# A window of eight loads on the loading queue of a squared-distance kernel

## The chip, the cores and the metric

One core of a Trainium2 chip. The metric is the device time of one execution in microseconds (us), which is some 1.35 us longer than the span of the profile. SP (SyncE) is the engine that here only waits and issues loads. A load counts as landed when the last of its 16 parts, which the trace records one by one, has arrived; a semaphore counts the parts up to 16.

## The reference

```python
x, y: float32 [1024, 4096]
np.sum((x - y) ** 2, axis=-1).astype(np.float32)     # 1024 results
```

33.55 MB are read once, 4 KB are written.

## The kernel before

Each of the 128 partitions holds eight rows of x and of y (8 x 4096 columns). SP issues 18 loads, cut into pieces of very different size; VectorE subtracts, ScalarE squares and sums. The buffers X and Y hold six rows each, so most of the loads from load 5 on reuse the place of rows 0 and 1, and SP issues them only when ScalarE has squared row 1.

```python
    H = 6 * D                                   # columns in each of the buffers X and Y
    xw = [4096, 12288, 8192, 5472, 1280, 960, 320, 160]
    yw = [16256, 8192, 2624, 2784, 1344, 480, 480, 288]
    late, last = 128, 192                       # two more small y loads, issued at the end
    ...
    def load(landed, src, dst, name, c0, c1):
        sem = prog.semaphore("%s%d" % (name, len(landed)))
        nc.sync.dma_start(out=dst[:, home(c0, c1)], in_=src[:, c0:c1]).then_inc(sem, 16)
        landed.append(((c0, c1), sem))
    ...
    todo = list(order)
    load(*todo.pop(0))
    prog.early(mybir.EngineType.SP)
    while todo and todo[0][5] <= H:             # the first block: loads 0 to 4
        load(*todo.pop(0))
    ...
            squared[piece] = n["acts"]
            if r in (0, 1):
                nc.sync.wait_ge(acts, n["acts"])
                while todo and todo[0][5] <= H + (r + 1) * D:
                    load(*todo.pop(0))
                if r == 1:                      # the second block: loads 5 to 17
                    while todo:
                        load(*todo.pop(0))
```

In issue order the loads have 2048, 6144, 8128, 4096 and 4096 KB (0 to 4), then 2736, 1312, 1392, 640, 672, 480, 240, 240, 160, 144, 80, 96 and 64 KB (5 to 17). Every load has its own semaphore, and VectorE waits for the loads of a piece before it subtracts.

## Time and profile before

| | before |
|---|---|
| median of the first 3 runs | 84.03 us (84.0 to 84.2) |
| span of the profile | 82.6 us |
| VectorE / ScalarE busy | 36.8 / 33.4 us |
| share of the span that the DMA engines are busy | 95.9% |
| last load landed | 80.25 us |

In the view of DMA issues, each line has the tensor, the issuing queue, the count, the size of one and the time from issue to landing; these are the lines for loads 13 to 17 of the kernel before:

```profile
X<-in_x_dram SPq DMA_DIRECT2D x1, 160.0 KB, 21.9
Y<-in_y_dram SPq DMA_DIRECT2D x1, 144.0 KB, 20.6
Y<-in_y_dram SPq DMA_DIRECT2D x1, 96.0 KB, 13.1
X<-in_x_dram SPq DMA_DIRECT2D x1, 80.0 KB, 15.6
Y<-in_y_dram SPq DMA_DIRECT2D x1, 64.0 KB, 12.8
```

A load of 64 KB that takes 12.8 us is not slow: it stands in a queue. The DMA row of the kernel before, for the stretch from 74 to 80.3 us alone (40 slices, busy tenths):

```profile
DMA  9999997999969999999899999999999999996000
```

There is work on the DMA engines up to 79.8 us. If the change lets the queue run empty, that row must show it.

### The profile page before, as it was taken

The page shows a single profiled execution, that of the slowest core. Times are in us where ns is not written, and L with a number is a line of the kernel's source. Part 1 is how long each engine was busy: PE and PEld are TensorE (multiplying, and loading weights), DVE is VectorE, ACT ScalarE, POOL GpSimd, SP SyncE. Part 2 cuts the span into 40 slices and gives each one's busy share as a digit, 9 for nine tenths or more (in the row PEclk, how much of TensorE's full clock was granted, in tenths as well). Part 3 has the DMA queues.
Part 4 walks back from the last instruction along what each step waited for, and adds up shares of the span by engine and source line. Part 5 has one row for each costly group of instructions (what it writes and reads, how often), then busy time and mean ns, then how long its engine had stood idle before and what let it go on. Part 6 is the DMA issues. An engine that isn't in the chain of part 4 may idle for free.

```text
span 82.6 us, 136 instructions
## 1 busy us (share of the span) xinstructions
DVE 36.8 (45%) x27; ACT 33.4 (40%) x41; POOL 0.2 (0%) x4
## 2 busy tenths in 40 slices
DVE  0000000000000000000299999999189996989992
ACT  3300000000000000000000979889896999899991
POOL 0000000000000000000000000000000000000000
DMA  5998998888999991999599699969979799999960
GB/s 127 389 500 381 595 547 381 381 381 381 504 504 504 504 504 63 441 504 504 254 508 508 286 476 508 476 286 508 423 339 509 339 437 440 426 402 416 395 220 2
DMA packets 2736, 33.56 MB, mean 406 GB/s; under 512 B 432, under 2 KB 1328, under 8 KB 1712
## 3 DMA queue, kind: packets, MB, share of 16 engines
q1 hardware_dynamic: 2736, 33.56, 95.9%
HBM read 33.55 MB, written 0.00 MB: 406 GB/s over the span
## 4 chain that ended last, share of the span: by engine, by line
DMA 63%; SPq 16%; DVE 12%; ACT 4%; issue 1%
DMA Y<-in_y_dram 63%; SPq L108 16%; DVE X L175 11%; ACT X L181 4%; DVE Y L204 0%; DVE results L188 0%; SPq L220 0%; DVE results L204 0%
## 5 line engine op out<-in xcount | busy, mean ns | idle before, releaser
L175 DVE TENSOR_TENSOR X<-X,Y 128x2048 f32<-128x2048 f32 (+10 forms) x21 | 36.2, 1780 | 44.3 <-DMA Y<-in_y_dram 44.3
L181 ACT ACTIVATE X<-X 128x2048 f32<-128x2048 f32 (+9 forms) x20 | 31.2, 1559 | 46.1 <-DVE X L175 46.0
L181 ACT ACTIVATION_READ_ACCUMULATOR X<-X 128x1 f32 x20 | 3.7, 186 | 0.0
L181 ACT ACT_TABLE_LOAD x1 | 1.3, 1283 | 1.4 <-PEq L19 1.4
L188 DVE TENSOR_REDUCE results<-parts 128x1 f32<-128x2 f32 (+2 forms) x4 | 0.4, 152 | 0.0
L204 DVE CUSTOM_DVE_ANT_0 Y<-X,parts 128x128 f32<-128x128 f32 x1 | 0.4, 352 | 0.0
L250 POOL MEMSET const-bfloat16-1.0<- 128x1 bf16 x1 | 0.1, 101 | 0.0
L250 POOL MEMSET const-uint8-127<- 128x1 uint8 x1 | 0.1, 101 | 0.0
L250 POOL MEMSET const-float32-0.0<- 128x1 f32 x1 | 0.1, 98 | 0.2 <-issue 0.2
L250 POOL MEMSET const-float32-1.0<- 128x1 f32 x1 | 0.1, 98 | 0.0
L204 DVE DVE_READ_ACCUMULATOR2_ANT results<- 128x1 f32 x1 | 0.1, 83 | 0.0
## 6 DMA issues: line engine op xcount, KB each, us to landing
Y<-in_y_dram SPq DMA_DIRECT2D x1, 8128.0 KB, 39.0
X<-in_x_dram SPq DMA_DIRECT2D x1, 6144.0 KB, 20.2
X<-in_x_dram SPq DMA_DIRECT2D x1, 4096.0 KB, 48.3
Y<-in_y_dram SPq DMA_DIRECT2D x1, 4096.0 KB, 57.5
X<-in_x_dram SPq DMA_DIRECT2D x1, 2736.0 KB, 13.3
X<-in_x_dram SPq DMA_DIRECT2D x1, 2048.0 KB, 7.1
Y<-in_y_dram SPq DMA_DIRECT2D x1, 1392.0 KB, 19.0
Y<-in_y_dram SPq DMA_DIRECT2D x1, 1312.0 KB, 16.1
```

Of the source, the lines that this page charges most:

```text
L108: nc.sync.dma_start(out=dst[:, home(c0, c1)], in_=src[:, c0:c1]).then_inc(sem, 16)
L175: nc.vector.tensor_sub(out=a, in0=a, in1=Y[:, home(c0, c1)]).then_inc(diffs, 1)
L181: nc.scalar.activation(out=a, in_=a, func=Square, accum_out=acc).then_inc(acts, 1)
L188: nc.vector.tensor_reduce(out=results[:, r : r + 1], in_=parts_of(r, len(row_parts[r])), axis=mybir.AxisListType.X, op=add,).then_inc(sums, 1)
L204: nc.vector.tensor_tensor_reduce(out=Y[:, home(*piece)], in0=X[:, home(*piece)], in1=X[:, home(*piece)], scale=1.0, scalar=parts_of(r, 1), ...
L250: nc = _bacc.Bacc("TRN2", target_bir_lowering=False, num_devices=1)
```

## The change

No load is issued before the load eight places ahead of it has landed. The intent is a bounded number of loads under way. Sizes, order, buffers and compute stay as they were.

```diff
-    landed_x, landed_y = [], []
+    landed_x, landed_y, issued = [], [], []
+
+    AHEAD = 8
     freed = []

     def load(landed, src, dst, name, c0, c1):
+        if len(issued) >= AHEAD:
+            nc.sync.wait_ge(issued[-AHEAD], 16)
         sem = prog.semaphore("%s%d" % (name, len(landed)))
+        issued.append(sem)
         nc.sync.dma_start(out=dst[:, home(c0, c1)], in_=src[:, c0:c1]).then_inc(sem, 16)
```

## The prediction

> **What bounds the kernel now.** I read the page first: engine shares, the 40 slices, the DMA part, the chain that ended last.
>
> ```profile
> DVE 36.8 (45%) x27; ACT 33.4 (40%) x41; POOL 0.2 (0%) x4
> DMA  5998998888999991999599699969979799999960
> q1 hardware_dynamic: 2736, 33.56, 95.9%
> HBM read 33.55 MB, written 0.00 MB: 406 GB/s over the span
> DMA 63%; SPq 16%; DVE 12%; ACT 4%; issue 1%
> ```
>
> VectorE and ScalarE are each under half busy; the 16 DMA engines are busy 95.9% of the span. The chain is mostly DMA. Its 16% of "SPq L108" look like an issue cost, so the question is whether SP's issuing holds anything up. The chain in order of time, from the second block of loads on, together with SP's timeline:
>
> ```profile
> 57.17 0.04 issue
> 57.22 1.69 SPq L108
> 58.91 0.04 issue
> 58.95 5.21 SPq L108
> 64.16 0.04 issue
> 64.20 2.69 SPq L108
> 66.89 0.04 issue
> 66.94 13.12 DMA Y<-in_y_dram
> 80.05 0.02 issue
> 80.08 0.57 DVE X L175 x2
> ```
>
> An ordinary issue takes 0.44 us (the timeline has 0.43 to 0.46 for those between 54 and 57 us). From 57.2 us on, single issues take 1.69, 5.21 and 2.69 us, and the line's own view gives 5.57 us for the last one. So SP is already being held: something in front of it is full. That is part of the chain only because the chain is followed through issues; the loads issued so late still wait 13 us for their turn. What counts is when each load lands. I number the 18 loads in issue order, 0 to 17, and add "us to landing" (DMA issues view; sizes identify the loads) to the issue's start (timeline):
>
> - 0 to 4 (2048, 6144, 8128, 4096, 4096 KB), issued in the first 3.2 us, land at 7.1, 21.7, 40.8, 50.6 and 60.3.
> - 5 (2736 KB) 53.45 + 13.3 = 66.8; 6 (1312) 53.8 + 16.1 = 69.9; 7 (1392) 54.3 + 19.0 = 73.3; 8 (640) 54.8 + 20.0 = 74.8; 9 (672) 55.3 + 21.1 = 76.4; 10 (480) 77.5; 11 (240) 78.2; 12 (240) 78.7; 13 (160) 79.1; 14 (144) 79.6; 15 (80) 64.2 + 15.6 = 79.8; 16 (96) 66.9 + 13.1 = 80.05; 17 (64) 67.4 + 12.8 = 80.2.
>
> They land strictly in issue order. Load 5 takes 66.8 - 60.3 = 6.5 us after load 4 for 2.80 MB, which is 431 GB/s; 6 and 7 take 3.1 and 3.4 us, about 420 to 430 GB/s; the small ones at the end fall towards 330 to 410 GB/s (loads 10 to 17, 1504 KB = 1.54 MB, between 76.4 and 80.2: 405 GB/s). The stretches by time agree: 437 GB/s from 41 to 53 us, 407 to 426 from 53 to 73. So one queue, served in order at its full rate, sets the end; after the last landings there are 0.57 us of subtraction, 0.35 us of the fused square and sum, the reduce, and the 1.4 us store.
>
> **What the Trainium skill says.** (1) "DMA: Bandwidth & Descriptors", section "Anatomy of one DMA — SWDGE (gpsimd) path": DMA engines do not wait on semaphores; a wait is held on the issuing sequencer ahead of dispatch, and the engines just consume their queues. So the added wait costs SP time and costs DMA time only if a queue runs empty. The trace agrees: SP stood at a wait for ACT for 50.2 us in all (the DMA queue's own waits) while DMA stayed at 9 tenths. (2) Same page, "Queues, rings and completion order": on each engine descriptors are consumed in ring order, but the 16 engines finish independently and completion is not promised in order. This matters, since a wait for a full landing is a wait for the slowest engine: with engines far apart, a quick one could empty its share of eight loads while a slow one holds the ninth back. The landing records of this trace show the 16 parts of one load within 0.2 to 0.25 us of each other (load 7: 73.01 to 73.25), in issue order, so there is no such spread. (3) Same page, "Specifications": fabric ceiling 435 GB/s. The trace shows 437 GB/s at best over 12 us, so the queue has no rate to gain. (4) Same page, "Latency and other measured facts": first byte of a hardware-issued DMA about 0.6 us. The trace bounds it from above: the 4 KB store took 1.4 us from issue to landing.
>
> **The change, part by part.** Nothing is removed; sizes, order, buffers and compute stay. Added: for loads 8 to 17, ten waits on SP, load i waiting for the landing of load i-8. SP computes nothing. Between the semaphore and the next instruction the chain shows 0.02 to 0.05 us, so ten satisfied waits would be about 0.4 us of SP time, off the path.
>
> When does each wait end, taking the landings above? Loads 0 to 3 have landed before the second block starts at 53.45, so loads 8, 9, 10 and 11 go as now. The others:
> - 12 waits for 4: 60.3 instead of 56.7.
> - 13 waits for 5: 66.8 instead of 57.2.
> - 14 waits for 6: 69.9 instead of 58.95.
> - 15 waits for 7: 73.3 instead of 64.2.
> - 16 waits for 8: 74.8 instead of 66.9.
> - 17 waits for 9: 76.4 instead of 67.4.
>
> So six loads are issued 3.6 to 11 us later. Does the queue run dry? Queue ahead at each of these moments, in KB: at 12, loads 5 to 11 = 2736 + 1312 + 1392 + 640 + 672 + 480 + 240 = 7472, 18 us of work; at 13, loads 6 to 12 = 4976; at 14, loads 7 to 13 = 3824; at 15, loads 8 to 14 = 2576; at 16, loads 9 to 15 = 2016, 5.0 us; at 17, loads 10 to 16 = 1440 KB = 1.47 MB, about 3.7 us (76.4 to 80.05). A new issue needs 0.44 us on SP and some start-up. Upper estimate for both: 1.4 us, the whole store. A more cautious one: load 0 took 7.1 us for 2.10 MB, where 435 GB/s would need 4.8, so 2.3 us of cold start. Load 17 is then in its queue by 77.8 (78.7 cautiously), and its turn comes at 80.05: margin 2.3 us (1.35). Load 16: in by 76.2 to 77.1, turn at 79.8, margin 2.7 or more. All earlier ones have more. So no landing moves.
>
> What is gained: the long issues. With at most eight loads in the queue the 1.69, 5.21, 2.69 and 5.57 us should all fall to about 0.44. (The long ones began with some ten loads outstanding: the 14th was issued with 4 to 12 ahead, the 18th finished at 73.0 with 8 to 16 and a piece of 7 ahead.) But this is SP time in which SP had nothing else to do; the next thing it does is the store at 81.18. Worth on the path: 0.
>
> Sum: DMA +0, VectorE and ScalarE +0, SP off the path, tail +0. 84.03 + 0.0, to which I add 0.02 for nothing more than the run spread of 84.0 to 84.2: **84.05 us**.
>
> **The rivals.**
> - *The queue runs dry at the end.* For it: the last loads are small, and waiting for a whole load's landing makes the window eight loads and not so many bytes. Against it: 1440 KB are still ahead at the tightest point. If the start-up were 5 us instead of at most 2.3, load 17 would land about 1.5 us late and the time would be 85 to 85.5; over 2% (1.7 us) would need more still. 3%.
> - *A shorter queue is served better*, because SP no longer pushes against a full one. For it: the rate falls from 437 GB/s (41 to 53 us, no issues) to 407 from 53 to 60 us when the second block is issued. Against it: rows get shorter there too, and the landings from 60 to 73 us, in the very time of the held issues, are at 420 to 431 GB/s. At the most the 1504 KB after 76.4 would go at 430 instead of 405 GB/s: 0.2 us, giving 83.8. A gain over 2% would need the whole stream above the best rate seen. 1%.
> - *A shorter queue is served worse*: engines that look ahead in their queue find less. Only the last few us have a short queue, and it is never empty; at the cost of, say, 5% over loads 10 to 17 (3.8 us) this is 0.2 us, giving 84.25. 10%.
>
> **Range and chances.** The mechanism says equal; the two small rivals are 0.2 us either way and the spread of runs 0.2 us. So 83.8 to 84.35. Faster by over 2% (under 82.35): 0.01. Within 2%: 0.97. Slower (over 85.7): 0.02.
>
> **What would show it.** In the profile after: issues of loads 12 to 17 start near 60.3, 66.8, 69.9, 73.3, 74.8 and 76.4, each about 0.44 us long, with no long SP issue left; their times to landing shrink to about 18, 12, 10, 6.5, 5 and 4 us (now 22, 22, 21, 16, 13 and 13) while the landings themselves stay within 0.3 us, the last near 80.2. The waits of SP show landings of DMA as releasers; the chain's "SPq L108" shrinks from 16% and DMA takes its place. Queue share stays near 96%, span near 82.6. Wrong if the DMA row shows a gap between 76 and 80 us, if load 17 lands over 4.5 us after its issue, or if the landings from 60 us on come at another rate than 420 to 431 GB/s.

## The result, and the profile after

After: 84.15 us median (84.07 to 84.24, six runs), before 84.13 us (84.0 to 84.2, six runs). The ratio is 1.0005, 95% interval 0.9992 to 1.0018. A ratio here is the mean time of one kernel's fast runs over that of the other's in the same rounds, so it is not quite the ratio of the medians.

The page of the kernel after: the DMA row of the whole span, the queue's share, the bytes, the chain that ended last.

```profile
DMA  5999999888999994799799899989999899999950
q1 hardware_dynamic: 2736, 33.56, 95.5%
HBM read 33.55 MB, written 0.00 MB: 405 GB/s over the span
DMA 78%; DVE 12%; ACT 4%; SPq 2%; issue 1%
```

The engines of the DMA are as full as they were. In the chain SP's queue fell from 16% to 2% and DMA rose from 63% to 78%, with no time gained: the chain only follows the last load back through another release, now a landing and not a string of issues.

SP's timeline after, loads 12 to 17 and the store (start, duration; "x2" merges two issues with what lies between, in the first line loads 11 and 12):

```profile
56.53 4.35 SPq L113 DMA_DIRECT2D Y<-in_y_dram  x2
67.03 0.33 SPq L113 DMA_DIRECT2D X<-in_x_dram  x1
70.19 0.33 SPq L113 DMA_DIRECT2D Y<-in_y_dram  x1
73.51 0.33 SPq L113 DMA_DIRECT2D X<-in_x_dram  x1
75.05 1.93 SPq L113 DMA_DIRECT2D Y<-in_y_dram  x2
81.44 0.35 SPq L237 DMA_DIRECT2D out_dram<-results  x1
```

The issues of 1.69, 5.21, 2.69 and 5.57 us are gone; each of these six loads is issued in 0.33 us (load 12 at 60.55, load 17 at 76.65 in the records). SP's waits, after:

```profile
SPq L113 <- DMA Y<-in_y_dram: 10.6, 4, 3.5
SPq L113 <- DMA X<-in_x_dram: 7.3, 2, 6.1
SPq L237 <- DVE results L193: 4.4, 1, 4.4
```

So 17.9 us of waits for landings (six waits) took the place of 13.4 us of holding: the four long issues less 0.44 us each. Where SP stands still has changed its name. The loads' times from issue to landing, after:

```profile
X<-in_x_dram SPq DMA_DIRECT2D x1, 160.0 KB, 12.4
Y<-in_y_dram SPq DMA_DIRECT2D x1, 144.0 KB, 9.6
Y<-in_y_dram SPq DMA_DIRECT2D x1, 96.0 KB, 5.2
X<-in_x_dram SPq DMA_DIRECT2D x1, 80.0 KB, 6.5
Y<-in_y_dram SPq DMA_DIRECT2D x1, 64.0 KB, 3.8
```

They fell by 8 to 11 us, and the end didn't move, because only the time that a load stands in the queue has shrunk. The DMA row from 74 to 80.3 us, after:

```profile
DMA  9999899999999999989999999999999999987310
```

No gap: the row stays at 8 or 9 up to 79.6 us and falls where that of before falls too. The landings, from the landing records (time at which the last of the 16 parts of a load landed):

| load | issued before | landed before | issued after | landed after | landing moved by |
|---|---|---|---|---|---|
| 0 | 0.00 | 7.12 | 0.00 | 7.36 | +0.24 |
| 4 | 2.77 | 60.27 | 2.81 | 60.53 | +0.26 |
| 7 | 54.30 | 73.25 | 54.56 | 73.50 | +0.25 |
| 9 | 55.26 | 76.38 | 55.57 | 76.64 | +0.26 |
| 12 | 56.73 | 78.75 | 60.55 | 79.00 | +0.25 |
| 15 | 64.20 | 79.79 | 73.51 | 80.02 | +0.23 |
| 17 | 67.41 | 80.25 | 76.65 | 80.46 | +0.21 |

The profiled execution after has a span of 82.9 us, 0.3 us more than before. That isn't the change: the 0.24 us stand already at load 0, which was issued long ahead of the first added wait, and they stay the same to the end. It is a difference between two executions, and the six runs of each kernel don't show it.

### The profile page after: what moved, and what is told of

It reads as the page before. It is cut to its first block, busy times and chain, and to the rows that moved or that the text cites. A ratio compares the mean times of both kernels' runs of the same rounds, so it can differ in the third digit from the quotient of the medians.

```text
span 82.9 us, 136 instructions
## 1 busy us (share of the span) xinstructions
DVE 36.8 (44%) x27; ACT 33.4 (40%) x41; POOL 0.2 (0%) x4
## 4 chain that ended last, share of the span: by engine, by line
DMA 78%; DVE 12%; ACT 4%; SPq 2%; issue 1%
DMA Y<-in_y_dram 54%; DMA X<-in_x_dram 24%; DVE X L180 11%; ACT X L186 4%; SPq L113 2%; DVE Y L209 0%; DVE results L193 0%; SPq L225 0%; DVE results L209 0%
```

## The experiments

The prediction rests on a margin: a late issue costs nothing as long as the work ahead of it outlasts its start-up. To test it I made the margin vanish in several ways, and worked out what each should cost by a recurrence: landing(i) = max(landing(i-1), landing(i-A) + S) + own time of i. Here A is the window, and the own times are the differences between the landings of before. S, the start-up, is what a load costs from its release to its landing beyond its own time. Four kernels ran first, four more and then two more later, all of them correct; the first eight ran on one chip and share most of their runs of before, the last two ran on another chip with new runs of before. Each ratio is against these runs of before (median 84.14 us for all).

**One load waits for the load just ahead.** AHEAD's lines are replaced:

```diff
-        if len(issued) >= AHEAD:
-            nc.sync.wait_ge(issued[-AHEAD], 16)
+        if len(issued) == 17:
+            nc.sync.wait_ge(issued[16], 16)
```

> Only load 17 (64 KB) waits, and for the landing of load 16, the load just ahead of it; loads 8 to 16 go without the added wait. Its queue is then empty, so its start-up S (from the semaphore that releases it to its first bytes arriving) lies open on the path. My theory (a wait costs DMA time only when the queue runs dry, S between 1.4 and 2.3 us): load 17 lands about 1.4 to 2.3 us later than now relative to load 16, the end by nearly as much (the reduce waits for load 17's piece): 85.4 to 86.3 us. Rival (later issue is hidden anyway, since the engines prefetch or the tail has slack): within 0.3 us of before.

Measured: 85.5 us, ratio 1.0167 (1.0143 to 1.0192), so 1.4 us more. Its chain has load 17 as

```profile
80.24 1.73 DMA Y<-in_y_dram
```

Load 17 was released at 80.22, when load 16 landed, and landed at 81.97; less its own 0.20 us, S is 1.55 us on an idle queue. The end moved by less than the landing, since VectorE's subtraction of load 16 was done meanwhile. The rival (late issues are hidden whatever is ahead) falls.

**Windows of 1, 2 and 4.** `AHEAD = 8` becomes 1, 2, 4.

> AHEAD = 1, one load at a time, each after the landing of the one before. My theory: 17 loads show S each: 17 x 1.4 = 24 us to 17 x 2.3 = 39 us more, 108 to 123 us; the gaps between landings each grow by the same S whether the load is big or small. Rival (a shorter queue is served better or worse in itself): the rate of the big loads 1 to 5 changes too, beyond the constant S.

Measured: 118.15 us, ratio 1.4055. From load 0 to load 17, 107.43 us pass and not 73.13: 34.3 us more over 17 loads, 2.0 us each. The chain of ahead_1, in order of time, three of its loads:

```profile
7.15 16.92 DMA X<-in_x_dram
...
96.55 3.13 DMA X<-in_x_dram
...
112.74 1.82 DMA Y<-in_y_dram
```

Load 1 (6144 KB, rows of 48 KB) takes 16.92 us and had 14.53 of its own: S is 2.4 us. Load 10 (rows of 3.75 KB): 3.13 less 1.16, 2.0 us. Load 17 (rows of 512 B): 1.82 less 0.20, 1.6 us. The total was as expected, but "the same S whether the load is big or small" was wrong: S grows with the length of the rows. No run was made to separate why, but the records of the packets (one packet is one row of one load) show where the growth sits. In each of loads 1 to 17 the first packet starts 0.94 to 0.97 us after the issue, and the landing comes 0.28 to 0.39 us after the end of the last packet, whatever the size. What grows is the time of the first 16 packets of a load, those after the pause: 2.5 us on average with rows of 48 KB, where the others take 1.8 us as in before; 0.35 us with 3.75 KB, where the median is 0.15; no more than the others with 512 B. So S is more than the wait for the first bytes, as which I had described it. As the later packets of the big loads keep their time, the rival (another rate for loads 1 to 5) falls.

> AHEAD = 2. My theory, by landing(i) = max(landing(i-1), landing(i-2) + S) + own time, own times from the landings of before: nothing lost up to load 8 or 9, then the small loads run dry: 3.2 us more at S = 1.4, 5.0 at 1.8, 7.5 at 2.3, so 87 to 91.5 us; loads 1 to 8 keep their landings. Rival (short queue is served at another rate): the landings of loads 2 to 8 move by over 0.3 us relative to load 0.

Measured: 90.68 us, ratio 1.0766 (1.0724 to 1.0808), 6.4 us more, which the recurrence gives for S a little over 2.0. Loads 1 to 6 keep their landings within 0.15 us (load 6: 70.12; before 69.92, of which 0.06 us were there at load 0). Loads 7 and 8 don't, against what I expected: less the 0.06 us they land 1.0 us later than in before, which is the sign I had set for the rival. Load 7 landed at 74.33, some 0.9 us late behind load 6, because four of its 16 parts came at 73.57 to 74.33 while twelve were in by 73.45. It had been issued 3.1 us ahead of its turn, so the recurrence has no loss there. In this profile, the slowest of the four runs (90.81 us, the fastest 90.03), load 17 lands 6.9 us later; with 0.9 us put on load 7 the recurrence gives that for S = 2.0, without it for 2.2. Why load 7 was late stays open.

> AHEAD = 4. My theory by the same recurrence: 0.5 us more at S = 1.4, 0.9 at 1.8, 1.4 at 2.3, all of it on loads 12 to 17: 84.6 to 85.5 us. No issue is held any more (all about 0.33 to 0.44 us). Rival (shorter queue is served better): under 84.0. Rival (window has slack to spare at four): equal to before within 0.15%.

Measured: 85.25 us, ratio 1.0136 (1.0112 to 1.016), 1.1 us more: S = 2.0. Its landings, less its 0.28 us at load 0, are those of before up to load 13; load 14 is 0.3 us late and loads 16 and 17 about 1.05, so the loss sets in two loads later than I had written. The DMA row from 74 to 82 us with the window of four:

```profile
DMA  9999999999899999999999959587745656400000
```

This is what a starved queue looks like: from the 24th slice (78.6 us) on the row thins to between four and nine tenths, and the end moves out. With the window of eight it stayed at 8 or 9 up to 79.6 us.

**The margin at its edge: load 17 waits for load 12.** Again in place of AHEAD's lines:

```diff
+        if len(issued) == 17:
+            nc.sync.wait_ge(issued[12], 16)
```

> Only load 17 waits, for load 12 (it landed at 78.75 in the profile of before; loads 13 to 16, 480 KB, 1.3 us of work, are then still ahead). With the start-up of 1.55 to 2.0 us that the runs with one waiting load and with windows of 1 and 4 showed, load 17 lands 0.25 to 0.7 us later; the subtraction of load 16 hides up to 0.3 us of that: end 0 to 0.4 us later, 84.1 to 84.6 us. This is the margin taken to its edge. Rival (a late issue costs the whole start-up whatever is ahead): 85.5 as when it waited for load 16.

Measured: 84.61 us, ratio 1.0057 (1.004 to 1.0074), 0.5 us more. That is just beyond my 0 to 0.4, and far from the 85.5 us of a full start-up. In the profile load 17 was released at 79.26 and landed at 81.41, so with 0.20 us of its own S is 1.95 us, at the top of what I had allowed; on the busy queue the start-up of this load was nearer 2.0 than the 1.55 of the idle one. (The profiled execution, 85.0 us, was the slowest of the seven; its load 4 was already late by 0.3 us more than its load 0.)

**Windows of 6 and 5.**

> AHEAD = 6. By the recurrence landing(i) = max(landing(i-1), landing(i-6) + S) + own time: 0.0 us more at S = 1.6, 0.1 at S = 2.0, 84.1 to 84.25 us; packets of every size take what they take in before. Rival (a shorter queue is served worse even while it is not empty): 84.5 or more.

Measured: 84.07 us, ratio 1.0000 (0.9981 to 1.002). Load 17 was issued at 78.26 and landed at 80.33, 0.08 us after before's, of which 0.03 stand at load 0. The records of the packets show the same median for every size of load row as before: 813 ns for 21,888 B, 79 ns for 1920 B, 27 ns for 512 B.

> AHEAD = 5. By the same recurrence 0.3 us more at S = 1.6, 0.7 at S = 2.0: 84.4 to 84.85 us, the loss in loads 14 to 17. Between ahead_4 (1.1 us more measured) and ahead_6. Rival (no sharp edge, the loss grows smoothly from 8 down): ahead_6 and ahead_5 lose alike.

Measured: 84.55 us, ratio 1.0052 (1.0033 to 1.007), 0.4 us more, on loads 16 and 17. So the edge is sharp: nothing at six, 0.4 us at five, 1.1 at four, 6.4 at two, 34 at one. The one recurrence gives 0 to 0.1, 0.5 to 0.7, 0.9 to 1.1 and 5.1 to 6.1 for the first four with S from 1.8 to 2.0: the measured times lie in or just beside these ranges, a little under at five, a little over at two, where load 7 was late.

**Does the number of loads count, or the work in them?** In the control split_free, loads 8 to 14 are each cut into two loads of half the columns, with AHEAD = 99 (no waits); split_6 is the same with AHEAD = 6.

```diff
+        number = len(landed_x) + len(landed_y)
+        mid = (c0 + c1) // 2
+        for a, e in [(c0, mid), (mid, c1)] if 8 <= number <= 14 else [(c0, c1)]:
+            if len(issued) >= AHEAD:
+                nc.sync.wait_ge(issued[-AHEAD], 16)
...          # one semaphore for each half; VectorE waits for both
```

> Control for split_6: loads 8 to 14 are each cut into two loads of half the columns, so the second block has 20 loads in place of 13; no added waits. Twice as many packets for these loads at some 8 ns each beyond their bytes (the 512 B packets take 27 ns where the rate of the large ones gives 19): 7 loads x 8 packets x 8 ns = 0.45 us more, so 84.3 to 84.8 us. SP's issues are held more often. Rival (the hold itself costs, being a window too): over 85.

> The same cut with AHEAD = 6. With whole loads a window of six lost nothing (ratio 1.000). If what counts is the work ahead of a late issue against a start-up of 1.8 to 2.0 us, six of the halved loads are too little: 0.6 to 0.85 us more than split_free by the recurrence. If the number of loads in flight counts (six are enough): the same as split_free within 0.15 us.

Measured: split_free 84.59 us (ratio 1.0054, interval 1.0039 to 1.0069), split_6 85.79 us (ratio 1.0188, interval 1.0169 to 1.0207). The control costs 0.45 us, as the extra packets should. The window of six, free with whole loads, costs 1.2 us more with halved ones. That is more than the 0.6 to 0.85 expected (the recurrence needs S = 2.2; no run shows why), but clear of zero. DMA rows from 74 to 83 us of the control and of the windowed one:

```profile
DMA  9999999999999999999999999995000000000030
```

```profile
DMA  9999999999999999999984885776646774000000
```

So the number of loads under way doesn't decide it: the same window of six is free or not according to the work that its loads hold.

**Are held issues free, or only free on SP?** The kernel before, with loads 5 to 17 issued by ScalarE's queue behind its square of row 1, no window:

```diff
-        nc.sync.dma_start(...)
+        q = nc.sync if len(landed_x) + len(landed_y) < 5 else nc.scalar
+        q.dma_start(...)
...
-                nc.sync.wait_ge(acts, n["acts"])
+                nc.scalar.wait_ge(acts, n["acts"])
```

> The kernel before, but loads 5 to 17 are issued by ScalarE's queue, behind its square of row 1, with no added waits. Tests the step that the held issues cost nothing because SP has nothing else to do. My theory: loads land as in before (last near 80.3), the issues are held there too until about 73 us, and ScalarE's squares, some 24.5 us of work that in before lie between 54 and 81 us, start only then: end near 73 + 24.5 + 2.5, so 97 to 101 us. If the hold is shorter on this queue: at least the 13 x 0.44 = 5.7 us of issuing stand ahead of the squares, 86 to 92 us. Rival (a held issue doesn't block its engine): 84 to 85 us.

Measured: 100.08 us, ratio 1.1907 (1.1873 to 1.194). Loads 5 to 17 land as in before (load 17 at 80.27); load 4, which now had loads of a second queue beside it, landed 2.5 us later than in before. Its chain in order of time, from load 13 on:

```profile
57.43 1.20 ACTq L109
58.63 0.03 issue
58.66 7.46 ACTq L109
66.12 0.03 issue
66.15 2.84 ACTq L109
68.99 0.03 issue
69.02 2.04 ACTq L109
71.06 0.03 issue
71.08 1.40 ACTq L109
72.48 0.05 issue
72.53 23.83 ACT X L182 x36
```

The holds look like SP's, 72.48 being the end of the last one, and here they stand in front of 23.83 us of squares that in before ran beside the landings. A held issue does block its engine here. On SP it was free because SP had nothing else to do before the store.

## Why the prediction was right, point by point

The time came out in the range, and the mechanism as forecast: the landings stayed, the waits moved, and none of the three signs of being wrong appeared (no gap from 76 to 80 us, load 17 landed 3.8 us after its issue, the landings from 60 us on at the old spacing). That I had written 0.02 us more and that 0.02 us more were measured is luck: both are far below the run spread of 0.2 us.

1. **"One queue, served in order at its full rate, sets the end."** Shown: once the 0.24 us of load 0 are taken off, the landings of before and after agree within 0.04 us, although the issues of loads 12 to 17 moved by 3.8 to 11.2 us. They came at 60.55, 67.03, 70.19, 73.51, 75.05 and 76.65, each some 0.25 us behind the forecast, which is again the late load 0.
2. **The margin.** I had 1.35 to 2.3 us for load 17 from a start-up of 1.4 to 2.3 us. The runs put the start-up near the end of a busy queue at about 1.8 to 2.0 us (2.2 fits split_6), so load 17, issued at 76.65, was in its queue by about 78.5 to 78.9 and its turn came at 80.26, when load 16 landed: 1.4 to 1.8 us of margin. The packets show the slack directly: after, the first packet of load 17 starts 2.64 us after the issue, while in ahead_1, with nothing ahead, it starts 0.95 us after, so some 1.7 us were spent in the queue. It is shown from the other side by the edge between six and five. Two of my readings were too kind. The store's 1.4 us, which I called an upper estimate, is less than every start-up measured, the 1.55 us on the idle queue too; the cautious 2.3 us carried the argument (and at a start-up of 5 us load 17 would be late by 1.35 us, not 1.5). And the 16 parts of a load, within 0.25 us of each other in before, are 0.6 us apart in after, still less than the margin.
3. **The long issues fall away and are worth nothing.** Right; each is 0.33 us and not the 0.44 I wrote, which is what an issue takes right behind another (0.43 to 0.46 in before). act_issues shows that they were worth nothing because they were on SP, and not because held issues cost nothing.
4. **Rival "a shorter queue is served better".** Not so: the packets' own times are unchanged, the sum of all packets over 16 engines is 79.4 us before and 79.3 after, and ahead_6 has the ratio 1.0000. The dip to 407 GB/s from 53 to 60.3 us that I named for it hangs on where the stretch is cut: from 53 to 60 us the same view of before has 425.
5. **Rival "a shorter queue is served worse".** Not while it holds work; it is true from a window of five down, by the start-up. The late parts of load 7 in ahead_2 and the 2.2 us that split_6 needs are not covered by this.
6. **"Ten satisfied waits would be about 0.4 us of SP time."** Too much: loads 8 to 11, whose waits were satisfied, are issued 0.48 to 0.50 us apart after and 0.48 to 0.49 before. It was off the path either way.

## What to carry to other kernels

When the transfer queue had work to the end, moving issues about moved only the time that loads spend waiting in it; look at landings, not at issues or at "us to landing". A cap on the loads under way was free as long as the work ahead of each late issue outlasted the start-up (some 2 us here, by estimate 0.9 MB at the 431 GB/s of the large loads), and that work must be counted in time, since six of the small loads at the end are enough and six of their halves are not. A held issue was free on SP, which had nothing else to do, and cost 16 us on ScalarE, which had: ask what stands behind it on its engine.

## What the Trainium skill lacked or had wrong

- "Perfetto Trace Analysis", section "What "DMA-bound" means", counts a sequencer track that is solid with DMA slices as a bound by the issuing sequencer. In before, SP's track is nearly solid from 53.45 to 72.98 us, and the change emptied it (0.33 us each) for a ratio of 1.0005: most of these slices were issues held while nine or more loads were under way, and they were not what bound the kernel.
- The same page, section "DMA Instruction — HWDGE (DVE, Sync)", has the profiled slice start after the semaphore wait; this agrees: the 17.9 us of waits lie between slices, the 13.4 us of holding within them. No page that I read gives a number for when an issue is held: here it began with nine loads ahead (loads 4 to 12; 1.69 us, then 5.21), with eight on ScalarE's queue (1.20, then 7.46), and at the same place with loads of half the size (1.66, then 5.32); yet load 16 went out in 0.43 us with ten ahead. The rule behind it stays open.
- "DMA: Bandwidth & Descriptors", section "Latency and other measured facts", gives about 0.6 us to the first byte for this kind of issue, and section "Anatomy of one DMA — SWDGE (gpsimd) path" a fixed 2.0 us for the other kind. The 0.6 agrees: in ahead_1 the first packet starts some 0.95 us after the start of the issue, 0.62 after its end. A load of this kind with nothing ahead costs 1.6 us (rows of 512 B) to 2.4 us (rows of 48 KB) beyond its own time, and load 17 of last_waits_12, on a busy queue, 1.95. That this grows with the row, by the first 16 packets after a pause, is on no page that I read.
- No page that I read has it that the 16 parts of a load keep their spread: 0.6 us at load 0 in after (6.75 to 7.36) and 0.6 us at load 17 (79.87 to 80.46), against 0.23 and 0.24 in before. The last part is late by the same 0.2 to 0.3 us in all the loads, and that accounts for the 0.24 us between the two profiles. It looks as if an engine that starts late stays late; the records of the parts don't name the engine, so this isn't shown.
